# A streaming-encoder layer on one core: carrying the pacing of DRAM sums in small ScalarE copies, and one more plain tile in the first up product

## The chip, the cores and the metric

One core of a Trainium2 chip runs the whole layer in one launch. The metric is the device time of an execution in microseconds (us); the text also uses the span of the profiled execution, from its first to its last instruction.

## The reference

One macaron layer over 512 tokens of width 1024, in float32: `x += 1/2 SwiGLU(rms(x))`, `x += Mix(rms(x))`, `x += 1/2 SwiGLU(rms(x))`, `x = rms(x)`. SwiGLU is

```python
def swiglu_ffn(x, w_gate, w_up, w_down):
    return (jax.nn.silu(x @ w_gate) * (x @ w_up)) @ w_down   # w_gate, w_up: 1024x2816, w_down: 2816x1024
```

`Mix` is one input projection, chunked attention (8 heads of 64) beside a pooling mixer, and an output projection. The change touches the two SwiGLU blocks alone.

## The kernel before

**Precision.** Every operand is split in a high part (a copy rounded by ScalarE, L141 to L143, L684) and a low part (the rest, a subtraction on VectorE, L147 to L149). A product is three matmuls: high by high, high by low, low by high (`mm3`, L217 to L219, or `mm_part`, L226, which issues one of the three).

**The up product** (`ffn_up`, called once for each SwiGLU) makes 22 tiles of 128 hidden columns, each a gate and an up column block. The first `PLAIN[i]` tiles (L38: 5 in the first product, 4 in the second) are plain: 48 matmuls of 512 columns. Of those the first two are interleaved over four banks (`first`), the others take two 512 KB weight loads each. After them every tile is made by a Strassen-like scheme: seven half-size products, 84 matmuls of 256 columns, with the tokens' side in seven prepared blocks (A11, S1, S3, S2, A12, A22, S4; `Norm.blocks`, L538 on) and the weights' side in sums built on VectorE (L969 to L973).

**The planner.** Plain tiles and the next `LISTED` (8) half-size tiles are put in a list of jobs with costs. `Work.latest` gives each job a time by which it must have started, counted back from the matmuls in their fixed order; that becomes the rank of all ScalarE and VectorE jobs (L298, L299). `Work.plan` then runs the list through and emits each engine's instructions in the order that comes out, with limited rooms: 8 banks, 8 temporaries `t` of 128x512, 4 places for split weights (`part`), 2 and 2 for raw weights. The remaining tiles (9 in the first product, 10 in the second) are written out by hand in a loop (from L1159 on). The low part that the first of these tiles needs first may end 0.9 us after the last listed matmul (L1133 to L1135).

**The down product** needs four sums of blocks of the down weights, made in DRAM before it: 48 transfers (a copy, then an accumulating one, for 4 sums and 6 groups), issued by GpSimd. They are cut into portions. `Down.make_sums` (L1291) issues one portion: a one-column copy by GpSimd of some tile (`mark`, L1298), so that the portion starts when that tile has been written, and then the portion's transfers (L1300). GpSimd runs in order, and an accumulating transfer waits for the one below it. In the first product the 28 portions follow `norm.rb`, blocks S3, A11, S2, A22 and S1 (L927 to L938), the activation `sg` of plain tiles 2 to 4 (L879), the tile `u` of every listed half-size tile (L1094), `u` of every hand-written tile (L1194), and two products of the down stage. The second product has 16 portions in the mixer and 20 in the up product, on plain tiles 2 and 3 and the other 18 tiles. `sg` and `u` are temporaries `t`: their place can't be written again before GpSimd's one-column copy has read it.

**The start.** In the first product ScalarE squares the tokens (`square`, L740 on) for the mean that the norm needs; the squares may start as soon as the tokens and the gains are there.

Of the kernel before, what the change touches and what calls it, by code (L numbers as in the profile page):

```python
# [8 lines left out]
F32 = mybir.dt.float32  # L9
# [25 lines left out]
RAW = 2  # L35
HILO = 3
SHIFT = 16
PLAIN = (5, 4)  # L38
LISTED = 8
PROBS = 3  # L40
EARLY = 16
LATE = 4
# [15 lines left out]
UP_HOP = 0.2  # L58
FIRST_BYTE = 1.8
RAW_LAG = 8.0  # L60
MORE = 6
MIX_ENGINES = {
    mybir.EngineType.PE, mybir.EngineType.DVE, mybir.EngineType.Activation, mybir.EngineType.Pool,
}
# [2 lines left out]
def layer(  # L67
# [44 lines left out]
    def name(what):  # L112
        n_tiles[0] += 1
        return f"{what}_{n_tiles[0]}"
# [123 lines left out]
    class Job:  # L238
        def __init__(self, no, engine, cost, rank, emit, after, gets, uses, lag, chunk):
            self.engine, self.cost, self.rank, self.emit = engine, cost, rank, emit  # L240
            self.after = [z for z in after if z is not None]
            self.gets, self.uses, self.lag, self.chunk = list(gets), list(uses), lag, chunk
            self.no, self.then, self.waits, self.ready = no, [], len(self.after), 0.0
            self.spare, self.seat, self.t0 = 0.0, 0.0, None

    class Work:

# [15 lines left out]
        def latest(self, rooms):  # L263


            t, users, first = 0.0, {}, {}
            row = sorted((z for z in self.jobs if z.engine == "pe" and z.rank >= 10.0), key=lambda z: z.rank)
            for z in row:
                z.by = t
                t += z.cost  # L270
            for z in self.jobs:
                for key in z.uses:
                    users.setdefault(key, []).append(z)
                for what, key in z.gets:
                    if key not in first.setdefault(what, {}):
                        first[what][key] = z
            further = {}
            for what, n in rooms.items():
                got = first[what]
                if what == "bank":  # L280
                    keys = sorted(got, key=lambda key: getattr(got[key], "by", got[key].seat))
                else:
                    keys = list(got)
                for key, later in zip(keys, keys[n:]):
                    for z in users.get(key, ()):
                        further.setdefault(z.no, []).append(got[later])

            def start_by(z):
                if not hasattr(z, "by"):
                    z.by = None  # L290
                    ends = [start_by(k) - (0.0 if k.engine == z.engine else self.hop) for k in z.then + further.get(z.no, [])]
                    end = min([*ends, t + z.spare])
                    z.by = end - z.cost - z.lag
                return z.by

            for z in self.jobs:
                start_by(z)
                if z.engine in ("act", "dve"):  # L298
                    z.rank = z.by  # L299
            return t  # L300

        def plan(self, room, free):
# [327 lines left out]
    def ffn_up(norm, wA, down, loaded, in_order, plain, turns=(), early=()):  # L630
# [109 lines left out]
        def square(k, before):  # L740
            def first():
                norm.acc = tpool.tile([P, S], F32, tag="acc", name=name("acc"), bufs=1)
                nc.scalar.activation(norm.acc, x[k], AF.Square)

            def emit():
                nc.scalar.activation(buf["sq", k], x[k], AF.Square)

            def add():
                nc.vector.tensor_tensor(norm.acc, norm.acc, buf["sq", k], op=ALU.add)

            if before is None:
                return job("act", 0.56, rank["acc"], first, [at_x[k], gain_in])
            z = job("act", 0.56, rank["acc"] + k, emit, [at_x[k]], [("t", ("sq", k))])
            return job("dve", 0.61, rank["acc"] + k, add, [z, before], uses=[("sq", k)])

        def chunk(kp):
# [90 lines left out]

        placed = {}

        def add_sums(f, done):  # L850
            k, second = down.pair(f)
            if second:
                job("dve", 0.78, rank["second"], lambda: down.sums(f), [done, placed[k]])
            placed[k] = done

        def evacuate(n, f, gate, up, after):
            g, sg = ("g", n), ("sg", n)
            z = job(
                "dve", 0.62, rank["evac"],
                lambda: nc.vector.tensor_tensor(  # L860
                    natural(buf[g]), ordered(buf[gate]), natural(norm.rb), op=ALU.mult
                ),
                [at_rb, *after], [("t", g)], [gate],
            )
            z = job(
                "act", 0.57, rank["evac"], lambda: nc.scalar.activation(buf[sg], buf[g], AF.Silu),
                [z], [("t", sg)], [g],
            )
            z = job(
                "dve", 0.61, rank["evac"],  # L870
                lambda: nc.vector.tensor_tensor(buf[sg], buf[sg], norm.rb, op=ALU.mult), [z],
            )
            done = job(
                "dve", 0.61, rank["place"], lambda: down.place(f, ordered(buf[up]), buf[sg]), [z],
                uses=[up, sg],
            )
            add_sums(f, done)
            if n >= 2:
                job("pool", 3.2, n, lambda: down.make_sums(buf[sg]), [done])  # L879

        for i in range(2):
            evacuate(i, down.order[i], ("first", 2 * i), ("first", 2 * i + 1), at_first[2 * i : 2 * i + 2])
# [7 lines left out]
            job("pool", 2.8, 0, lambda k=k: put_aside(buf["turned", k], k), [z], uses=[("turned", k)], lag=3.5)  # L890

        freed = [None] * KD
        for n in range(2, plain):
            f, lows = down.order[n], []
            for j in range(2):
                key = ("W", n, j)
                kind = ("praw", "wraw")[j % 2 == 0]
                z = load(wA[2 * f + j], lambda key=key: buf[key][:, :1024], 0.45, 1.3, [(kind, key)])
                lows.append(
                    split_jobs(key, lambda key=key: buf[key][:, :1024], 1024, rank["plain"], [z], [key])  # L900
                )
            units = [(k, j) for k in range(KD) for j in range(2)]
            if n < plain - 1:
                units.sort(key=lambda u: u[1])
            last = [None] * 2
            for k, j in units:

                def unit(n=n, k=k, j=j):
                    w = buf["part", ("W", n, j)]()
                    mm3(buf["plain", n, j], cut(w, k * P, P), norm.h[k], k == 0, k == KD - 1)  # L910

                last[j] = job(
                    "pe", 0.648, filler(), unit, [lows[j][1], last[j]],
                    [("bank", ("plain", n, j))], [("part", ("W", n, j))],
                )
                if n == plain - 1 and j:
                    freed[k] = last[j]
            evacuate(n, f, ("plain", n, 0), ("plain", n, 1), last)
# [5 lines left out]
        used = {k: [turned[k]] if k in turned else [] for k in range(KD)}  # L924
        at_a = norm.blocks(down.pool, aside, work, at_rb, used, freed)

        if not loaded:  # L927
            for i, (z, after) in enumerate(
                (
                    (at_rb, lambda: norm.rb),  # L930
                    (at_a[S3][0][0], lambda: work.buf["whole", S3][0][:, 0].bitcast(F32)),
                    (at_a[A11][0][0], lambda: norm.a[A11][0][0].bitcast(F32)),
                    (at_a[S2][0][0], lambda: work.buf["whole", S2][0][:, 0].bitcast(F32)),
                    (at_a[A22][0][0], lambda: norm.a[A22][0][0].bitcast(F32)),
                    (at_a[S1][0][0], lambda: norm.a[S1][0][0].bitcast(F32)),
                )
            ):
                job("pool", 3.2, 1 + 0.1 * i, lambda after=after: down.make_sums(after()), [z])  # L938

        raws, w = {}, {}  # L940

# [84 lines left out]
        def operands(n):  # L1026
# [2 lines left out]
            raw = ("raw", n)  # L1029
            at_raw = job(  # L1030
                "sp", 0.9, n_loads[0] + n, lambda: fetch_into(buf[raw], down.order[n]), [],
                [("praw", raw)], lag=2.6 if n < plain + 2 else RAW_LAG,
            )

            def made(i, src, cols, deps, uses):
# [20 lines left out]
        def half_tile(n):  # L1056
# [34 lines left out]

            p = multiply(acc, 11, 0, A11, True, [])
            u_lo = read(u, 0, acc, 1.0, [p])
            job("pool", 3.2, n, lambda: down.make_sums(buf[u][:, :HT]), [u_lo])  # L1094
            p = multiply(up_hi, 13, S, S3, True, [])
            z_hi = read(z, 1, up_hi, -1.0, [p])
            p = multiply(acc, 24, 0, S2, False, [u_lo])
# [136 lines left out]
    class Down:  # L1234
# [56 lines left out]
        def make_sums(self, after):  # L1291

            at = self.n_sums
            self.n_sums += 1
            part = self.steps[self.bounds[at] : self.bounds[at + 1]]
            with tc.manual_schedule(engines={mybir.EngineType.Pool}):
                mark = small.tile([P, 16], F32, tag="mark", name=name("mark"))
                nc.gpsimd.tensor_copy(mark[:, 0:1], after[:, 0:1])  # L1298
                for _, at, i, g in part:
                    nc.gpsimd.dma_start(  # L1300
                        self.rows(i, g), self.rows(self.terms[i][at], g),
                        **(dict(accum_op=ALU.add) if at else {}),
                    )
# [1258 lines left out]
```

## Time and profile before

| | us |
|---|---|
| median of 3 runs | 806.54 (806.04 to 808.33) |
| profiled execution, its own time | 802.69 |
| span of that execution | 800.9 |

A row of the page or of a list of groups gives engine, line, operation and shape, then busy time and what ended the idle time before. A row of a timeline gives start, duration, engine and line; a bracket at its end is the idle time just before it and what ended it. TensorE is PE, its weight loads PEld, VectorE DVE, ScalarE ACT, GpSimd POOL.

### The profile page before, as it was taken

The page shows a single profiled execution, that of the slowest core. Times are in us where ns is not written, and L with a number is a line of the kernel's source. Part 1 is how long each engine was busy: PE and PEld are TensorE (multiplying, and loading weights), DVE is VectorE, ACT ScalarE, POOL GpSimd, SP SyncE. Part 2 cuts the span into 40 slices and gives each one's busy share as a digit, 9 for nine tenths or more (in the row PEclk, how much of TensorE's full clock was granted, in tenths as well). Part 3 has the DMA queues.
Part 4 walks back from the last instruction along what each step waited for, and adds up shares of the span by engine and source line. Part 5 has one row for each costly group of instructions (what it writes and reads, how often), then busy time and mean ns, then how long its engine had stood idle before and what let it go on. Part 6 is the DMA issues. An engine that isn't in the chain of part 4 may idle for free.

```text
span 800.9 us, 14970 instructions
## 1 busy us (share of the span) xinstructions
PE 790.1 (99%) x5706; PEld 746.2 (93%) x5706; DVE 712.4 (89%) x1117; ACT 498.7 (62%) x858; POOL 158.5 (20%) x246
## 2 busy tenths in 40 slices
PE   9999999999999999999999999999999999999996
PEld 7889899999999999888888888899999999988986
DVE  7899899999988998777699799999999999986997
ACT  7556565555666665557769555455666555766584
POOL 0035321122220000232254245021110011200010
PEclk9999999999999999999999999999999999999998
DMA  8469977698898765585655867145774467869642
GB/s 298 149 170 308 284 214 196 164 240 198 227 280 288 219 201 162 173 264 117 163 191 107 185 178 212 57 151 194 174 186 165 159 173 176 260 238 339 215 140 106
DMA packets 73992, 158.57 MB, mean 198 GB/s; under 512 B 6576, under 2 KB 31680, under 8 KB 73536
## 3 DMA queue, kind: packets, MB, share of 16 engines
q1 hardware_dynamic: 49952, 109.09, 40.3%
q0 software_dynamic: 23680, 48.24, 28.1%
q8 instruction: 45, 0.74, 0.4%
q10 hardware_dynamic: 288, 0.27, 0.1%
q14 instruction: 27, 0.22, 0.1%
HBM read 153.38 MB, written 50.34 MB: 254 GB/s over the span
## 4 chain that ended last, share of the span: by engine, by line
PE 85%; DVE 2%; DMA 1%; issue 1%; ACT 0%; SPq 0%; ACTq 0%; DVEq 0%
PE mm L217 12%; PE mm L219 12%; PE mm L218 12%; PE mm L226 10%; PE a L218 9%; PE a L217 9%; PE a L219 9%; PE a L226 6%; DMA raw<-wsum 1%; PE mm L2005 1%; PE mm L2095 1%; PE a L2069 1%; DVE parts L147 1%; PE mm L2069 0%; PE a L2095 0%
## 5 line engine op out<-in xcount | busy, mean ns | idle before, releaser
L147 DVE TENSOR_TENSOR parts<-raw,parts 128x1024 fp32r<-128x1024 f32 (+2 forms) x129 | 137.3, 1078 | 14.3 <-ACT parts L141 12.2
L1018 ACT ACTIVATE t<-mm 128x256 f32<-128x256 f32 x93 | 35.8, 385 | 86.6 <-PE mm L219 59.7
L141 ACT CAST parts<-raw 128x1024 fp32r<-128x1024 f32 (+1 forms) x60 | 59.3, 993 | 32.7 <-DMA raw<-wsum 10.3
L1298 POOL COPY mark<-t 128x1 f32<-128x1 f32 x40 | 24.9, 622 | 268.1 <-DVE t L1193 149.5
L1300 POOL DMA_DIRECT2D wsum<-in_wB_dram x72 | 73.0, 1146 | 12.6 <-DMA wsum<-wsum 7.5
L684 ACT CAST parts<-raw 128x1024 fp32r<-128x1024 f32 (+2 forms) x69 | 59.8, 883 | 17.8 <-PE a L218 8.0
L147 DVE TENSOR_TENSOR wlo<-raw,whi 128x1024 fp32r<-128x1024 f32 (+1 forms) x41 | 46.8, 1141 | 6.3 <-ACT whi L141 4.3
L147 DVE TENSOR_TENSOR ah<-acts,ah 128x512 fp32r<-128x512 f32 (+1 forms) x72 | 47.1, 663 | 3.0 <-ACT ah L141 2.9
L141 ACT CAST ah<-acts 128x512 fp32r<-128x512 f32 (+1 forms) x72 | 41.0, 583 | 8.6 <-PE mm L218 6.1
L219 PE MATMUL mm<-ha,parts 128*128 128x256 f32 x152 | 41.9, 276 | 0.8 <-DVE parts L147 0.8
L1598 DVE TENSOR_TENSOR parts<-raw,parts 128x1024 fp32r<-128x1024 f32 x24 | 29.6, 1239 | 14.7 <-ACT parts L1593 14.7
L217 PE MATMUL mm<-ha,parts 128*128 128x256 f32 x152 | 41.8, 275 | 0.0
L218 PE MATMUL mm<-ha,parts 128*128 128x256 f32 x152 | 41.8, 275 | 0.0
L1593 ACT CAST parts<-raw 128x1024 fp32r<-128x1024 f32 x24 | 25.2, 1048 | 25.9 <-PE a L218 7.1
L226 PE MATMUL mm<-ha,parts 128*128 128x256 f32 x312 | 38.6, 275 | 0.0
L217 PE MATMUL mm<-ah,parts 128*128 128x256 f32 x136 | 37.4, 275 | 0.0
L218 PE MATMUL mm<-ah,parts 128*128 128x256 f32 x136 | 37.4, 275 | 0.0
L219 PE MATMUL mm<-ah,parts 128*128 128x256 f32 x136 | 37.4, 275 | 0.0
L226 PEld LDWEIGHTS mm<-ha,parts 128*128 128x128 f32 x312 | 36.8, 192 | 0.1
L1018 ACT ACTIVATE t<-a 128x256 f32<-128x256 f32 x47 | 18.1, 384 | 29.5 <-PE a L226 21.2
L963 DVE TENSOR_TENSOR parts<-wsum,parts 128x1024 fp32r<-128x1024 f32 x26 | 31.7, 1219 | 2.6 <-ACT parts L958 2.6
L226 PE MATMUL a<-ha,parts 128*128 128x256 f32 x264 | 32.6, 275 | 0.0
(410 smaller groups left out, 3013.6 us busy)
## 6 DMA issues: line engine op xcount, KB each, us to landing
raw<-in_wA_dram SPq DMA_DIRECT2D x86, 512.0 KB, 5.1
wsum<-in_wB_dram POOLq DMA_DIRECT2D x60, 512.0 KB, 7.7
raw<-wsum SPq DMA_DIRECT2D x36, 512.0 KB, 4.9
raw<-in_wB_dram SPq DMA_DIRECT2D x30, 512.0 KB, 4.9
wsum<-wsum POOLq DMA_DIRECT2D x20, 512.0 KB, 4.8
x<-in_xT_dram SPq DMA_DIRECT2D x16, 256.0 KB, 5.3
raw<-in_wQK_dram SPq DMA_DIRECT2D x8, 512.0 KB, 4.1
wsum<-in_wB_dram POOLq DMA_DIRECT2D x12, 256.0 KB, 7.6
```

What stands on the lines that cost most here:

```text
L141: nc.scalar.copy(hi, src)
L147: nc.vector.tensor_tensor(lo, src, hi.bitcast(F32), op=ALU.subtract)
L217: nc.tensor.matmul(acc, a[0], high, start=start, stop=False, **more)
L218: nc.tensor.matmul(acc, a[0], low, start=False, stop=False, **more)
L219: nc.tensor.matmul(acc, a[1], high, start=False, stop=stop, **more)
L226: nc.tensor.matmul(acc, a[1 if i == 2 else 0], moved, start=start, stop=stop, **more)
L684: "act", c_high, rank_of, lambda: nc.scalar.copy(pair()[0], src()),
L963: nc.vector.tensor_tensor(lo, src, hi.bitcast(F32), op=ALU.subtract)
L1018: nc.scalar.activation(natural(dst), ordered(src), AF.Copy, scale=scale)
L1300: nc.gpsimd.dma_start(self.rows(i, g), self.rows(self.terms[i][at], g), **(dict(accum_op=ALU.add) if at else {}),)
L1593: return lambda: nc.scalar.copy(buf["part", i][0], buf["raw", i])
L1598: nc.vector.tensor_tensor(lo, buf["raw", i], hi.bitcast(F32), op=ALU.subtract)
```

## The change

Portions of the sums no longer read a temporary or a block. ScalarE copies one column of the tile in question to a tile of its own (`pace`, ring of 4), at once when that tile is written, and GpSimd's copy reads that. In the first product the portions now follow the high parts of seven weight tiles of the plain tiles (all but the first) and blocks S3, S2, A22 and S1; the three on `sg`, and those on `norm.rb` and A11, are gone. In the second they follow the high parts of the gate weights of plain tiles 2 and 3. `MORE` 7 for 6 makes 29 portions of the 28 in the first product. `PLAIN` becomes (6, 4) and `LISTED` 7: the first product has 6 plain, 7 listed and 9 hand-written tiles, the second 4, 7 and 11. Smaller parts: jobs of the norm's mean, of the tokens' split, of the squares and of the second to fourth weight tile rank 10 us earlier; the first two squares wait for split weights; the raw loads of the first two half-size tiles are planned with the same lag of 8.0 us as the others; `mark` has 8 columns, not 16.

```diff
-PLAIN = (5, 4)
-LISTED = 8
+PLAIN = (6, 4)
+LISTED = 7
...
-MORE = 6
+MORE = 7
+EARLY_MEAN = 10.0
...
                 if z.engine in ("act", "dve"):
-                    z.rank = z.by
+                    z.rank = -1e3 if z.at_once else z.by - EARLY_MEAN * (z.rank < -5.0 and z.rank >= -19.0)
...
             if before is None:
-                return job("act", 0.56, rank["acc"], first, [at_x[k], gain_in])
-            z = job("act", 0.56, rank["acc"] + k, emit, [at_x[k]], [("t", ("sq", k))])
+                return job("act", 0.56, rank["acc"], first, [at_x[k], at_w[0][0][0]])
+            then = at_w[0][3][0] if k == 1 else None
+            z = job("act", 0.56, rank["acc"] + k, emit, [at_x[k], then], [("t", ("sq", k))])
...
+        def pace(at, order, src):
+
+            n = next(paces)
+
+            def note():
+                buf["pace", n] = small.tile([P, 1], F32, tag="pace", name=name("pace"), bufs=4)
+                nc.scalar.copy(buf["pace", n], src())
+
+            z = job("act", 0.22, rank["copy"], note, [at])
+            z.at_once = True
+            job("pool", 3.2, order, lambda: down.make_sums(buf["pace", n]), [z])
...
             add_sums(f, done)
-            if n >= 2:
-                job("pool", 3.2, n, lambda: down.make_sums(buf[sg]), [done])
...
-        if not loaded:
-            for i, (z, after) in enumerate(
...
-                job("pool", 3.2, 1 + 0.1 * i, lambda after=after: down.make_sums(after()), [z])
+        at_weights = [z for pair in plain_lows[(0 if loaded else 1) :: (2 if loaded else 1)] for z in pair[:1]]
+        if loaded:
+            for i, (z, what) in enumerate(zip(at_weights, plain_keys[::2])):
+                pace(z, i, lambda what=what: buf["part", what](0, 0)[0][:, 0:1].bitcast(F32))
+        else:
+            for i, (z, what) in enumerate(zip(at_weights, plain_keys[1:])):
+                pace(z, i, lambda what=what: buf["part", what](0, 0)[0][:, 0:1].bitcast(F32))
+            for i, what in enumerate((S3, S2, A22, S1)):
+                pace(at_a[what][0][0], 10 + i, lambda what=what: norm.a[what][0][0][:, 0:1].bitcast(F32))
...
-                [("praw", raw)], lag=2.6 if n < plain + 2 else RAW_LAG,
+                [("praw", raw)], lag=RAW_LAG,
...
-            job("pool", 3.2, n, lambda: down.make_sums(buf[u][:, :HT]), [u_lo])
+            pace(u_lo, 20 + n, lambda: buf[u][:, 0:1])
...
-                mark = small.tile([P, 16], F32, tag="mark", name=name("mark"))
+                mark = small.tile([P, 8], F32, tag="mark", name=name("mark"))
```

## Rows read from the trace of the kernel before

**Rows 1.** The page: busy time of each engine, and its share of the span.

```profile
PE 790.1 (99%) x5706; PEld 746.2 (93%) x5706; DVE 712.4 (89%) x1117; ACT 498.7 (62%) x858; POOL 158.5 (20%) x246
```

**Rows 2.** Who TensorE waited for, whole span: us in total, times, longest.

```profile
PE mm L226 <- ACT t L1018: 1.9, 1, 1.9
PE a L448 <- DVE less_ln L432: 1.1, 1, 1.1
PE mm L219 <- DVE parts L147: 0.8, 1, 0.8
PE mm L226 <- ACT parts L684: 0.3, 1, 0.3
```

**Rows 3.** Stages: length, busy us (instructions) by engine, granted clock, DMA share, GB/s.

```profile
26.80:57.90 31.10, 31.10 (x146) 27.22 (x144) 29.87 (x38) 16.14 (x22) 8.65 (x12) 1.00 0.53 153
84.00:87.00 3.00, 1.11 (x10) 0.92 (x9) 1.52 (x3) 1.78 (x5) 2.51 (x6) 1.00 1.07 340
87.00:134.80 47.80, 47.80 (x430) 47.80 (x430) 46.55 (x70) 29.34 (x52) 12.60 (x16) 1.00 0.92 249
136.40:221.00 84.60, 84.60 (x758) 84.60 (x759) 80.13 (x113) 50.70 (x93) 17.09 (x26) 1.00 0.80 203
525.00:600.00 75.00, 75.00 (x674) 75.00 (x673) 71.27 (x102) 45.59 (x82) 15.95 (x22) 1.00 0.65 185
600.00:694.00 94.00, 94.00 (x843) 93.97 (x843) 88.79 (x126) 57.44 (x105) 12.82 (x22) 1.00 0.60 180
780.00:800.90 20.90, 14.47 (x99) 13.39 (x98) 15.77 (x48) 9.25 (x22) 0.00 (x0) 0.89 0.26 101
```

**Rows 4.** The chain that ended last: start, us, matmuls of 256 columns, then of 512.

```profile
107.11 6.70 PE mm L226 x60
...
489.23 15.11 PE mm L226 x70
```

**Rows 5.** Timeline of 77 to 91 us, all engines: before and after TensorE's longest stall.

```profile
77.05 2.48 POOL L1300 DMA_DIRECT2D wsum<-in_wB_dram  x1
...
84.49 0.51 POOL L1300 DMA_DIRECT2D wsum<-wsum  x1 [4.96 <-DMA wsum<-in_wB_dram]
84.98 0.20 POOL L1298 COPY mark<-t 128x1 f32<-128x1 f32 x1
...
85.22 0.42 ACT L1109 ACTIVATE t<-t 128x256 f32<-128x256 f32 x1 [3.96 <-POOL mark L1298]
85.54 0.60 ACT L684 CAST parts<-raw 128x512 fp32r<-128x512 f32 x1
...
86.75 1.60 PE L226 MATMUL mm<-sa,parts 128*128 128x256 f32 x12 [1.89 <-ACT t L1018]
```

**Rows 6.** Timelines of VectorE, then TensorE, at the end of the listed tiles.

```profile
134.13 0.42 DVE L1316 TENSOR_TENSOR acts<-acts 128x256 f32<-128x256 f32 x1
...
135.59 0.68 DVE L147 TENSOR_TENSOR parts<-raw,parts 128x512 fp32r<-128x512 f32 x1
136.19 1.22 DVE L147 TENSOR_TENSOR wlo<-raw,whi 128x1024 fp32r<-128x1024 f32 x1
...
136.32 0.38 PE L219 MATMUL mm<-ha,parts 128*128 128x256 f32 x1 [0.85 <-DVE parts L147]
```

**Rows 7.** Timelines of ScalarE and TensorE, 17 to 40 us: casts, first plain matmul, one-column activation.

```profile
18.66 1.03 ACT L684 CAST parts<-raw 128x1024 fp32r<-128x1024 f32 x1
...
26.82 0.38 PE L217 MATMUL a<-hhi,parts 128*128 128x512 f32 x1
...
30.08 0.20 ACT L441 ACTIVATE table<-t 128x1 f32<-128x1 f32 x1
...
37.16 1.05 ACT L684 CAST parts<-raw 128x1024 fp32r<-128x1024 f32 x1 [3.95 <-PE a L218]
```

**Rows 8.** DMA issues of 44 to 100, then 0 to 44 us: count, KB, us to landing.

```profile
wsum<-in_wB_dram POOLq DMA_DIRECT2D x15, 512.0 KB, 9.0
raw<-in_wA_dram SPq DMA_DIRECT2D x8, 512.0 KB, 7.3
...
raw<-in_wA_dram SPq DMA_DIRECT2D x12, 512.0 KB, 4.7
```

**Rows 9.** GpSimd's timeline, 0 to 260 us: the first portions of the sums.

```profile
29.34 1.11 POOL L1298 COPY mark<-rb 128x1 f32<-128x1 f32 x1 [27.54 <-DVE rb L534]
...
44.17 0.63 POOL L1298 COPY mark<-xa 128x1 f32<-128x1 f32 x1 [12.88 <-ACT xa L143]
```

**Rows 10.** Timeline of 0 to 10 us: TensorE and its weight loads at the start.

```profile
5.06 0.30 PEld L226 LDWEIGHTS mm<-hlo,parts 128*128 128x128 f32 x2 [0.24 <-DVE hlo L149]
...
7.83 0.48 PE L226 MATMUL mm<-hhi,parts 128*128 128x512 f32 x1 [0.34 <-ACT parts L684]
...
8.17 0.19 PEld L226 LDWEIGHTS mm<-hlo,parts 128*128 128x128 f32 x1 [0.16 <-DVE hlo L149]
```

**Rows 11.** VectorE's timeline around the end of the second product's listed tiles.

```profile
580.10 0.42 DVE L1086 TENSOR_TENSOR t<-a,t 128x256 f32<-128x256 f32 x1 [0.57 <-PE a L226]
...
598.54 0.68 DVE L147 TENSOR_TENSOR parts<-raw,parts 128x512 fp32r<-128x512 f32 x1
```

## What the change will do to the time

> **What bounds the kernel now.** I read the page's busy shares first. TensorE is busy 790.1 us of a span of 800.9, VectorE 89%, ScalarE 62%, GpSimd 20% [rows 1]. So the time is the sum of the matmuls plus 10.8 us in which TensorE stands still, and the next view is who it waited for [rows 2]: 1.9 us for ScalarE's reading of a bank (L1018), 1.1 before its first instruction, 0.8 for a low part from VectorE, 0.3 for a first cast. Third, the stages [rows 3]: the last 20.9 us hold 14.47 busy, so 6.43 of the idle time lies at the very end, out of the change's reach; 84 to 87 us has 1.11 busy of 3.00; the stretches beside it, and the whole of the second product's half-size tiles (525 to 694), are full. What the change can win is therefore bounded: 1.89 + 0.85 + 0.34 = 3.08 us. What it costs has to be looked for in matmuls, and in new stalls.
>
> **The longest stall, step by step** [rows 5]. GpSimd issues a transfer in 77.05 to 79.53, stands 4.96 us until one has landed, issues the accumulating one at 84.49, and only then makes its one-column copy (84.98). ScalarE's SiLU at L1109 wants a temporary `t` and waits 3.96 us for that copy. Behind it on ScalarE, which goes in order, stand a cast (85.54) and the bank readings L1116 and L1018; TensorE gets its bank at 86.75, having lost 1.89. So of a ScalarE wait of 3.96, 3.96 - 1.89 = 2.07 us was covered.
>
> **The other stall** [rows 6]. The third matmul of the first hand-written tile needs a 512-column low part; VectorE makes it at 135.59, after sums of activations (L1316) and other work, and TensorE loses 0.85. VectorE had been busy 46.55 of 47.80 us before that [rows 3]: it was late by its load.
>
> **The change, part by part.**
>
> *One half-size tile becomes a plain one.* Matmuls of 256 columns follow each other in 6.70 / 60 = 0.1117 us, those of 512 in 15.11 / 70 = 0.2159 [rows 4]. A half-size tile is 84 x 0.1117 = 9.38, a plain one 48 x 0.2159 = 10.36. The swap adds **0.98 us** to a TensorE that is full. The second product's swap is of a listed for a hand-written tile with the same 84 matmuls: 0. [...]
>
> *The portions' new source.* With `pace`, no temporary and no block waits for GpSimd any more in the listed tiles, so the wait of 3.96 has no cause left: **-1.89**. Bounds 0 (another late reader takes its place) and -1.89. I take the whole, since the copy's end at 85.18 is what stands right before the SiLU's start at 85.22.
>
> *What the copies cost ScalarE.* The first product gets 7 + 4 + 7 = 18, the second 2 + 7 = 9. A one-column activation takes 0.20 us [rows 7]: 27 x 0.20 = 5.4 us on an engine that is 29.34 of 47.80 busy among the half-size tiles [rows 3], so one copy in a tile lies in idle time: 0. If that cover went, a bank reading would be 0.20 late behind each copy. GpSimd gets one portion, so one `mark`, more; its transfers stay 48. Behind a copy that waits for its place in the ring of 4 stands all of ScalarE; that is a rival below.
>
> *When the transfers run.* The first portions come at 29.34 and 44.17 now [rows 9]; after the change they follow casts that are made from 18.66 on, at the first four intervals up to 37.16 one in 4.6 us [rows 7], so some seven portions run before 50 us, in a stretch where the DMA engines are only 0.53 busy [rows 3]. They share them with SP's weight loads. Where both were dense a weight load took 7.3 us to land [rows 8]. Plain weights are cast well ahead of use (18.66, the first matmul of their tile at 26.82 [rows 7]), so 0 on the path; between 0 and 7.3 - 4.7 = 2.6, if a load took that instead of the 4.7 of the first 44 us [rows 8] and nothing covered it. In exchange the pile-up of 60 to 85 us gets thinner.
>
> *VectorE's load.* A half-size tile takes it 46.55 x 9.38 / 47.80 = 9.13 us [rows 3]. A plain one takes two low parts of 1.22 and three operations of 512 columns at 0.68 [rows 6]: 4.48. The swap frees 4.65 us. The hand-over comes at 134.8 - 1.89 + 0.98 = 133.9, so 0.9 earlier, and VectorE was 0.85 late: 4.65 - 0.91 - 0.85 leaves 2.9 us of room if the freed time can be used. Part of it may fall before the tokens' blocks exist, when there is nothing to do. So between 0 and **-0.85**; I take the whole. The plain tile also puts 10.36 us between the start and the first half-size tile, which can only help the blocks.
>
> *Hand-over in the second product.* It comes a tile earlier, at some 590.7. VectorE waited 0.57 us for TensorE at 580.10, so it had no arrears there, and its low part for the hand-over at 600.1 was made from 598.54 to 599.22 [rows 11]. I take 0, between 0 and +0.85, the stall of the first product.
>
> *The start.* The first squares move behind casts. TensorE's 0.34 at 7.83 was ended by such a cast [rows 10]; but its next weight load at 8.17, like that at 5.06, waited for a low part of the tokens from VectorE, which nothing moves. So 0, between 0 and -0.34. Earlier ranks for the norm's mean make `rb` earlier; no TensorE wait hangs on it [rows 2]: 0. The lag of 8.0 and the narrower `mark`: 0, no row has a wait that they would move.
>
> **Sum**: 0.98 - 1.89 - 0.85 = -1.76 us. Against the profiled execution's 802.69 that is 800.9; the median of the runs shown is 806.54, 3.85 above it, and -1.76 on that gives **804.8**. That is 0.22%; about 0.3%, 2.4 us, is what a measurement of this kernel can tell from no change.
>
> **Rivals.**
>
> *Only the GpSimd stall goes.* VectorE's freed time falls into the plain tiles, where its work waits for raw weights and for places, and the 0.85 stays: 0.98 - 1.89 = -0.91, 805.6. For it: VectorE is 96% busy in 26.8 to 57.9 only while blocks are made [rows 3], and these keep their place beside the last plain tile. Against it: the second product, with one tile more in its list, had no such stall [rows 3].
>
> *It doesn't do what it says.* The releaser in the trace is inferred; if the temporary was late for another reason as well, the 1.89 stays: 0.98 - 0.85 = +0.13, 806.7, or with both stalls +0.98, 807.5. Against it: those 0.04 us between the copy's end and the SiLU [rows 5].
>
> *More is won.* The start's 0.34 as well, and in the executions that aren't profiled a wait for GpSimd that is longer than the 3.96 here, since it hangs on when transfers land: every further microsecond of it counts in full, as the 2.07 of cover are used up. With 0.34 and half a microsecond: -2.6, 803.9.
>
> *Slower: ScalarE waits for the ring.* A `pace` copy can't be written before GpSimd has read the one four before. Portions come every 4.6 us in the plain tiles [rows 7], and a portion whose accumulating transfer waits for one just issued takes up to a landing, 9.0 us [rows 8]. While such portions alternate with free ones GpSimd is two to three portions behind; from four on ScalarE stands. One whole landing, less the cover of 2.07 seen above, is 6.9 us: -1.76 + 6.9 = +5.2, 811.7. Against it: the cover is larger among plain tiles, whose casts are 8 us ahead. [...]
>
> **Chances.** Forecast 0.42, only one stall gone 0.13, nothing gone 0.15, more won 0.18, ring 0.12. The forecast's own range, with a microsecond of spread between medians, is 803.5 to 806.2. The range to the neighbours, leaving out most of the ring's case and the tail of the gains, is **802.6 to 808.6**. Faster by over 0.3% takes a third of the forecast, most of "more won" and little else: 0.32. Slower: the ring and a part of "nothing gone": 0.17. Within 0.3%: 0.51.
>
> **What would show it.** TensorE's instructions fall by 36 and its busy time rises by about 1; no TensorE wait for L1018 near 85 to 97 us, no ScalarE wait for `mark`; GpSimd's first `mark` near 19 us; no wait for `parts` at the hand-over near 134 us; nothing new at 590. Wrong would be: a ScalarE wait for `mark` at the pace copies, a TensorE stall among plain tiles 3 to 5 for weights, or one at 590.

## The result, and the profile after

The changed kernel takes 811.57 us (median of six runs, 809.93 to 812.73), the kernel before 806.04 beside it (median of five): a ratio of 1.0065 (95% interval 1.0042 to 1.0088), 0.65% slower. Two slow executions far outside the rest, one of 888.49 us of the kernel before and one of 1672.07 us in the last experiment below, are left out of the medians. The forecast was 804.8, in a range of 802.6 to 808.6.

First the waits of TensorE in the profile after, the view of [rows 2], and the first line of the page:

```profile
PE 794.6 (98%) x5670; PEld 747.4 (92%) x5670; DVE 709.0 (87%) x1111; ACT 501.8 (62%) x878; POOL 154.3 (19%) x247
```

```profile
PE mm L219 <- DVE parts L1612: 7.0, 1, 7.0
PE a L449 <- DVE less_ln L433: 1.1, 1, 1.1
PE a L219 <- DVE wlo L148: 0.8, 1, 0.8
PE mm L227 <- ACT parts L685: 0.3, 1, 0.3
PE mm L220 <- DVE parts L148: 0.3, 1, 0.3
PE a L518 <- DVE t L829: 0.2, 1, 0.2
```

(Line numbers are those of the changed kernel, some 1 to 14 further on; L1612 is the mixer's low part, `low_part`.) Of the two stalls that the prediction wanted to remove, the 1.89 at the bank reading is off the list, and of the 0.85 at the hand-over 0.3 is left (L220 waiting for `parts`, at 135.13 us). New is one of 7.0 us in a stage that the change doesn't touch: the mixer, which begins after the first down product.

The timeline of TensorE after, at the mixer's start (L218 to L220 on `parts,hhi` are its first matmuls, L518 on `m,mean_of` is a later landmark):

```profile
323.16 0.38 PE L218 MATMUL mm<-parts,hhi 128*128 128x512 f32 x1
330.50 0.80 PE L219 MATMUL mm<-parts,hhi 128*128 128x512 f32 x1 [6.95 <-DVE parts L1612]
331.09 0.63 PE L220 MATMUL mm<-parts,hlo 128*128 128x512 f32 x1
334.93 0.54 PE L220 MATMUL mm<-parts,hlo 128*128 128x512 f32 x1
335.30 0.38 PE L218 MATMUL mm<-parts,hhi 128*128 128x512 f32 x1
346.31 0.59 PE L518 MATMUL a<-m,mean_of 128*128 128x512 f32 x2
```

The same landmarks before:

```profile
323.80 0.38 PE L217 MATMUL mm<-parts,hhi 128*128 128x512 f32 x1
337.40 0.59 PE L517 MATMUL a<-m,mean_of 128*128 128x512 f32 x2
```

The reader sees where 10.0 us of span (810.9 against 800.9) come from. At the mixer's first matmul the changed kernel is 323.80 - 323.16 = 0.64 *ahead*. From there to the landmark it takes 23.15 and not 13.60, 9.55 more: the stall of 6.95, and the eleven matmuls from 330.50 to 335.30, which take 4.80 where 11 x 0.2159 [rows 4] = 2.37 would do. The windows say why those are slow (columns: stretch, its length, busy and instructions, granted clock, share of DMA, GB/s):

```profile
328.00:330.00 2.00, 0.00 (x0) 0.60 0.00 0
332.00:334.00 2.00, 2.00 (x6) 0.50 0.87 285
335.00:336.00 1.00, 1.00 (x6) 0.88 0.35 143
```

The rest, 1.09, comes later; 0.79 of it is the wait of `wlo` at 749.65.

**Who was late.** ScalarE and VectorE at the mixer's start, after (L1607 is the mixer's cast, L1612 its low part; L1428 adds a product to the tokens, L512 sums their squares):

```profile
321.91 1.05 ACT L1607 CAST parts<-raw 128x1024 fp32r<-128x1024 f32 x1 [7.31 <-PE a L219]
322.69 1.43 DVE L1428 SCALAR_TENSOR_TENSOR x<-a,x 128x256 f32<-128x256 f32 x4 [6.93 <-PE a L220]
328.62 0.69 DVE L512 TENSOR_TENSOR acc<-acc,t 128x512 f32<-128x512 f32 x1
329.23 2.35 DVE L1612 TENSOR_TENSOR parts<-raw,parts 128x1024 fp32r<-128x1024 f32 x2
```

and before:

```profile
317.19 1.05 ACT L1593 CAST parts<-raw 128x1024 fp32r<-128x1024 f32 x1 [1.43 <-PE a L218]
318.27 1.23 DVE L1598 TENSOR_TENSOR parts<-raw,parts 128x1024 fp32r<-128x1024 f32 x1 [1.72 <-ACT parts L1593]
319.87 1.05 ACT L1593 CAST parts<-raw 128x1024 fp32r<-128x1024 f32 x1 [1.63 <-PE a L218]
320.95 1.23 DVE L1598 TENSOR_TENSOR parts<-raw,parts 128x1024 fp32r<-128x1024 f32 x1 [1.45 <-ACT parts L1593]
323.33 1.43 DVE L1414 SCALAR_TENSOR_TENSOR x<-a,x 128x256 f32<-128x256 f32 x4 [1.16 <-PE a L219]
```

Before, two of the mixer's weights are split while TensorE still does the down product, and the tokens' sums come behind them. After, the first cast waits 7.31 us for a matmul of the down product to let its place go, and the low part stands on VectorE behind the tokens' work of 322.69 to 329.23.

**Theory P, the places.** Split weights go round in four places: the mixer's three of `parts_sb` and one in a pool. A plain tile asks for two of them, a half-size one for four, and the down product goes on from where the up product stopped. Counted in the code, the tiles and the down product ask 120 times before, 118 times after. 120 is a multiple of four and 118 is two off, so after the change the last down weights lie in other places. The mixer always begins with places 0, 1, 2. Before, the weight in place 0 was the first of the last ones to be used up; after, it is one of the last two. **Rival L:** the mixer's loads or the portions are late by the new timing. In the profile after, no transfer runs at all from 322 to 331 (a share of 0.00 in every window there), so the loads are not merely slow; but they too wait for room, and the rows alone don't separate cause from effect.

### The profile page after: what moved, and what is told of

Its sections match the earlier page's. It is cut to its first block, busy times and chain, and to the rows that moved or that the text cites. A ratio compares the mean times of both kernels' runs of the same rounds, so it can differ in the third digit from the quotient of the medians.

```text
span 810.9 us, 14852 instructions
## 1 busy us (share of the span) xinstructions
PE 794.6 (98%) x5670; PEld 747.4 (92%) x5670; DVE 709.0 (87%) x1111; ACT 501.8 (62%) x878; POOL 154.3 (19%) x247
## 4 chain that ended last, share of the span: by engine, by line
PE 92%; DVE 4%; DMA 2%; ACT 1%; issue 1%; SPq 0%; DVEq 0%; ACTq 0%
PE mm L220 13%; PE mm L218 13%; PE mm L219 13%; PE mm L227 12%; PE a L218 10%; PE a L220 10%; PE a L219 10%; PE a L227 8%; DMA wsum<-wsum 1%; PE mm L2019 1%; PE mm L2109 1%; PE a L2083 1%; DVE parts L148 1%; DMA raw<-in_wA_dram 1%; DVE parts L977 1%
## 5 line engine op out<-in xcount | busy, mean ns | idle before, releaser
L1032 ACT ACTIVATE t<-mm 128x256 f32<-128x256 f32 x88 | 33.9, 386 | 86.3 <-PE mm L220 63.0
L142 ACT CAST parts<-raw 128x1024 fp32r<-128x1024 f32 (+1 forms) x62 | 61.2, 993 | 33.6 <-PE mm L219 10.9
L685 ACT CAST parts<-raw 128x1024 fp32r<-128x1024 f32 (+2 forms) x65 | 56.2, 885 | 24.3 <-PE a L219 10.9
L977 DVE TENSOR_TENSOR parts<-wsum,parts 128x1024 fp32r<-128x1024 f32 x36 | 43.9, 1220 | 5.0 <-ACT parts L972 5.0
L1607 ACT CAST parts<-raw 128x1024 fp32r<-128x1024 f32 x24 | 25.1, 1046 | 35.2 <-PE a L219 11.1
L1312 POOL COPY mark<-pace 128x1 f32<-128x1 f32 x27 | 14.8, 548 | 161.9 <-ACT pace L858 161.9
L148 DVE TENSOR_TENSOR wlo<-raw,whi 128x1024 fp32r<-128x1024 f32 (+1 forms) x37 | 41.9, 1133 | 3.9 <-ACT whi L685 2.2
L1612 DVE TENSOR_TENSOR parts<-raw,parts 128x1024 fp32r<-128x1024 f32 x24 | 29.4, 1232 | 18.2 <-ACT parts L1607 18.2
L220 PE MATMUL mm<-ha,parts 128*128 128x256 f32 x160 | 44.2, 276 | 0.2
L218 PE MATMUL mm<-ha,parts 128*128 128x256 f32 x160 | 44.0, 275 | 0.0
L219 PE MATMUL mm<-ha,parts 128*128 128x256 f32 x160 | 44.0, 275 | 0.0
L220 PE MATMUL mm<-ah,parts 128*128 128x256 f32 x148 | 40.8, 276 | 0.3 <-DVE parts L148 0.3
L218 PE MATMUL mm<-ah,parts 128*128 128x256 f32 x148 | 40.7, 275 | 0.0
L219 PE MATMUL mm<-ah,parts 128*128 128x256 f32 x148 | 40.7, 275 | 0.0
L1312 POOL COPY mark<-t 128x1 f32<-128x1 f32 x20 | 6.1, 303 | 166.4 <-DVE t L1207 166.4
L1032 ACT ACTIVATE t<-a 128x256 f32<-128x256 f32 x48 | 18.5, 386 | 28.5 <-PE a L227 20.2
L972 ACT CAST parts<-wsum 128x1024 fp32r<-128x1024 f32 x36 | 35.7, 1044 | 0.0
```

Source lines behind the costliest of these rows:

```text
L142: nc.scalar.copy(hi, src)
L148: nc.vector.tensor_tensor(lo, src, hi.bitcast(F32), op=ALU.subtract)
L218: nc.tensor.matmul(acc, a[0], high, start=start, stop=False, **more)
L219: nc.tensor.matmul(acc, a[0], low, start=False, stop=False, **more)
L220: nc.tensor.matmul(acc, a[1], high, start=False, stop=stop, **more)
L685: "act", c_high, rank_of, lambda: nc.scalar.copy(pair()[0], src()),
```

## The experiments

**The mixer's places alone.**

```diff
+        own_places = (2, 0, 1)
         def part_at(slot):
-            return parts_sb[:, slot * 2112 :][:, :1024], ...
+            at = own_places[slot] * 2112
+            return parts_sb[:, at:][:, :1024], ...
...
-            own_order[kp] = work.slot_of["part", "up", kp][1]
+            own_order[kp] = own_places[work.slot_of["part", "up", kp][1]]
```

> The changed kernel, but the mixer takes its first three split weights' places in the order 2, 0, 1 instead of 0, 1, 2 (place 2 holds the down weight that is multiplied earliest of those left, place 0 one that is multiplied nearly last). Theory P (places: with one half-size tile fewer the rotation of four places ends two further on, so the mixer's first cast asks for a place that the down product still reads): ScalarE's first mixer cast comes near 317 to 319 us instead of 321.9 behind a wait of 7.3, TensorE's stall of 6.95 at 330.5 is below 1.5, the clock of 0.50 to 0.69 behind it is gone (some 2.3 us), and the time falls by 7 to 9.5, to 802 to 804.5. Rival L (the mixer's loads, or the portions, come late by the new timing): the cast still waits 5 us or more and the time stays within 1.5 of 811.6.

Measured: 803.57 us (803.14 to 804.17), 0.9972 of the kernel before (0.9958 to 0.9986; its median beside it 806.06), 8.0 below the changed kernel. Its timeline:

```profile
315.70 1.05 ACT L1610 CAST parts<-raw 128x1024 fp32r<-128x1024 f32 x1 [1.96 <-PE a L219]
321.06 1.05 ACT L1610 CAST parts<-raw 128x1024 fp32r<-128x1024 f32 x1 [4.31 <-PE a L219]
328.38 2.35 DVE L1615 TENSOR_TENSOR parts<-raw,parts 128x1024 fp32r<-128x1024 f32 x2
329.65 0.48 PE L219 MATMUL mm<-parts,hhi 128*128 128x512 f32 x1 [1.78 <-DVE parts L1615]
```

One permutation of three places takes the loss away. The stall of 1.78 that remains (expected: below 1.5) belongs to the second weight: its cast is over at 322.11, but its low part stands behind the tokens' sums until 328.38. Rival L falls.

**The copies without the plain tile.** The changed kernel with the tile numbers of before:

```diff
-PLAIN = (6, 4)
-LISTED = 7
+PLAIN = (5, 4)
+LISTED = 8
...
-MORE = 7
+MORE = 6
```

> The changed kernel with the numbers of before: five plain and eight listed half-size tiles in the first product, six listed portions; the small copies, the portions' new sources and the edits at the start stay. Theory P: the places end as before, so no TensorE stall above 1 at the mixer's start; the 1.89 is still gone, the start's 0.73 stays: about -1.2 against the kernel before, 804 to 806 timed (profiled 801 to 802). Rival L, the portions or the new copies make the mixer late: a stall of 5 to 7 near 330 and 810 to 813.

Measured: 801.18 us (800.80 to 801.85), 0.9952 of the kernel before (0.9935 to 0.9968): the fastest so far, and more than either theory gave. Its waits of TensorE hold no mixer:

```profile
PE a L449 <- DVE less_ln L433: 1.1, 1, 1.1
PE a L219 <- DVE wlo L148: 0.7, 1, 0.7
PE mm L220 <- DVE parts L148: 0.4, 1, 0.4
```

On the profile's scale, 799.0 against 800.9, the gain is about the 1.89 of the prediction. On the scale of the timed runs it is 806.06 - 801.18 = 4.88. The difference lies in the kernel before, not in this one (below).

**The plain tile without the copies.** The kernel before with the tile numbers of after:

```diff
-PLAIN = (5, 4)
-LISTED = 8
+PLAIN = (6, 4)
+LISTED = 7
```

> The kernel before with six plain and seven listed half-size tiles in the first product and nothing else of the change: no small copies, portions still follow the temporaries. Theory P: the stall of the changed kernel appears, 5 to 7 us before the mixer's first weights and some 2 us of half and 0.69 clock behind it, ScalarE's first mixer cast near 322 behind a wait of TensorE; 811 to 815 timed. Rival L: no such stall; the swap's 0.98 alone or less, 805.5 to 807.5.

Measured: 811.87 us, 1.0087 (1.0067 to 1.0106). Two of its four waits of TensorE, its first mixer cast, GpSimd's longest wait in the listed tiles, and all that ScalarE waits for GpSimd:

```profile
PE mm L218 <- DVE parts L1598: 7.0, 1, 7.0
PE mm L226 <- DVE parts L147: 0.3, 1, 0.3
```

```profile
321.49 1.05 ACT L1593 CAST parts<-raw 128x1024 fp32r<-128x1024 f32 x1 [7.32 <-PE a L218]
88.11 0.51 POOL L1300 DMA_DIRECT2D wsum<-wsum  x1 [8.25 <-DMA wsum<-in_wB_dram]
```

```profile
ACT t L1018 <- POOL mark L1298: 0.2, 1, 0.2
```

The stall comes with the tile and needs none of the copies. What was not expected: its list of waits has no bank reading (L1018) any more, so the long stall of before goes without any copy. GpSimd itself is no earlier: it stands 8.25 us and reads a `t` at 88.61, later than the kernel before at its stall (84.98 [rows 5]), but ScalarE waits only 0.2 us for a `mark`. Why that late reading holds up nothing here isn't shown; the order of the portions has changed (the first two that read a `t` come at 55.87 and 59.29, before at 65.46 and 73.27). The two parts of the change remove the same stall; their gains do not add up, and with the copies on top (811.57) the kernel is no faster than with the tile alone.

**A second profile of the kernel before**, unchanged.

> The kernel before, unchanged, for a second profile: its unprofiled runs (803.99 to 808.33) are longer than its profiled 802.69, and the trace does not show where. If the mixer's start is what varies, this profile has a stall above 1 us near 331 with a lower clock behind it and a time between 803 and 808; if the difference is spread or lies at the end, no single new stall above 0.5.

Measured: 806.77 us, a span of 805.0. Waits of TensorE:

```profile
PE mm L226 <- ACT t L1018: 3.8, 1, 3.8
PE a L448 <- DVE less_ln L432: 1.1, 1, 1.1
PE mm L219 <- DVE parts L147: 0.7, 1, 0.7
PE a L226 <- ACT t L1018: 0.2, 1, 0.2
```

GpSimd's wait ahead of the first of these, and windows behind it (it ends at 89.58):

```profile
87.31 0.51 POOL L1300 DMA_DIRECT2D wsum<-wsum  x1 [6.76 <-DMA wsum<-in_wB_dram]
```

```profile
90.00:92.00 2.00, 2.00 (x11) 0.50 0.94 318
92.00:94.00 2.00, 2.00 (x18) 0.87 1.10 249
```

Neither expectation held: there is one longer stall, but at the bank reading, not at the mixer. It is the stall of [rows 5], 3.80 and not 1.89, because GpSimd stands 6.76 us on the landing of the transfer below, not 4.96. Behind this stall the granted clock was 0.50, in the window of 90 to 92; behind the 1.89 of [rows 2] it was 1.00 [rows 3]. From the first half-size tile to the mixer this execution takes 327.85 - 58.19 = 269.66, that of the prediction 323.80 - 57.90 = 265.90. Of the 3.76 more, 1.92 are stalls (3.80 + 0.18 + 0.68 against 1.89 + 0.85) and 1.84 are left. The lower clock shows in 1.28 of these: the first 12 matmuls behind the stall take 92.30 - 89.58 = 2.72 us here, and 88.19 - 86.75 [rows 5] = 1.44 in the profile of the prediction. This execution first, then that one:

```profile
89.58 2.93 PE L226 MATMUL mm<-sa,parts 128*128 128x256 f32 x12 [3.80 <-ACT t L1018]
92.30 0.94 PE L226 MATMUL mm<-ha,parts 128*128 128x256 f32 x6
```

```profile
88.19 1.50 PE L226 MATMUL mm<-ha,parts 128*128 128x256 f32 x12
```

So the profile on which the prediction rested was a mild execution of before. In this one the two stalls at the bank reading and these 1.84 come to 3.80 + 0.18 + 1.84 = 5.82, three times the 1.89.

**Before, with unfavourable places.** In the kernel before, `own_places = (2, 1, 0)` with the other edits of the first experiment, so that nothing but the place of the mixer's weights moves.

> The kernel before with the mixer's places in the order 2, 1, 0 instead of 0, 1, 2 and nothing else, so that its first split weight asks for the place whose down weight is multiplied nearly last. Nothing before the mixer moves. Theory P: ScalarE's first mixer cast waits for TensorE to within 2 us of the down product's end, TensorE stalls 3 to 7 us at the mixer's first weights and its clock falls behind it; 809 to 814. Rival (the changed kernel's stall came with the plain tile in another way, by timing or load): no stall above 1, 805 to 807.

Measured: 808.16 us (805.52 to 811.43), 1.0034 of before (1.0014 to 1.0055; its median beside it 805.21). The profiled execution, 811.43, is the longest of the ten; it has stalls of 3.97 and 1.02 at the bank reading as well. Timeline of the mixer's start:

```profile
327.17 2.00 ACT L1596 CAST parts<-raw 128x1024 fp32r<-128x1024 f32 x2 [6.79 <-PE a L218]
329.29 1.22 DVE L1601 TENSOR_TENSOR parts<-raw,parts 128x1024 fp32r<-128x1024 f32 x1
330.56 0.48 PE L218 MATMUL mm<-parts,hhi 128*128 128x512 f32 x1 [1.76 <-DVE parts L1601]
336.94 0.48 PE L218 MATMUL mm<-parts,hhi 128*128 128x512 f32 x1 [0.93 <-DVE parts L1601]
```

The cast is as late as after the change (a wait of 6.79), with every tile as before: the place makes it late. But the time is below the 809 of the expectation, TensorE loses 1.76 + 0.93 = 2.69, not 6.95, and its matmuls from 330.88 to 335.63 follow each other in 4.75 / 22 = 0.2159 us, the pitch of [rows 4]. Here VectorE has the first low part right behind the tokens' products and ahead of the sums; after the change it stood behind both. A late place alone costs some 3 us here (808.16 - 805.21 = 2.95). The rest of the changed kernel's loss goes with VectorE's other order; that the order makes it, and what gives the build that order, isn't shown.

**Seven plain tiles.** Two half-size tiles made plain against before ask for 2 x (4 - 2) = 4 places fewer: a whole turn.

```diff
-PLAIN = (6, 4)
-LISTED = 7
+PLAIN = (7, 4)
+LISTED = 6
...
-MORE = 7
+MORE = 8
```

> The changed kernel with seven plain and six listed half-size tiles (one portion more, as it has one more source). Two half-size tiles fewer than before shift the rotation by four places, a whole turn. Theory P: no stall above 1 at the mixer's start; against the kernel with five plain tiles and the same copies (801.18) two swaps more at 0.98 less a hand-over stall of 0.40 that goes: 802 to 803.5, faster than the changed kernel by 8 or more although it has one slower tile more. Rival (a plain tile more makes the mixer late): stall of 7 or more, 812 to 814.

Measured: 802.13 us (801.83 to 803.93), 0.9962 of before (0.9947 to 0.9978), 9.4 below the changed kernel with one costly tile more. All of its waits of TensorE:

```profile
PE a L449 <- DVE less_ln L433: 1.1, 1, 1.1
```

Six tiles stall at the mixer, five and seven don't: a plain tile more is not by itself what makes the mixer late; the phase in which it leaves the ring is. Against five tiles this is +0.95; the two swaps at 0.98, less the stalls of 0.40 and 0.69 that stood in the one profile of five, are +0.87.

**The copies of the listed tiles alone.** The kernel before with `pace`, a `mark` of 8 columns and this line:

```diff
-            job("pool", 3.2, n, lambda: down.make_sums(buf[u][:, :HT]), [u_lo])
+            pace(u_lo, n, lambda: buf[u][:, 0:1])
```

> The kernel before with small copies for the listed half-size tiles alone (and the mark of 8 columns, which makes the room for them); other sources, tiles and start as before. If the long stall hangs on GpSimd holding the temporaries u of listed tiles: no TensorE wait for the bank reading, a hand-over stall of 0.4 to 0.9 stays, 801 to 802.5. If the early portions on weights and the edits at the start carry the gain instead: the stall of 2 to 4 stays and the time is 805 to 807.

Measured: 805.58 us, 1.0011 (0.9996 to 1.0027), no gain. The stall is as in the second profile of before (L1032 is its bank reading, L1123 the SiLU):

```profile
87.22 0.51 POOL L1314 DMA_DIRECT2D wsum<-wsum  x1 [6.44 <-DMA wsum<-in_wB_dram]
87.72 0.20 POOL L1312 COPY mark<-t 128x1 f32<-128x1 f32 x1
87.96 0.42 ACT L1123 ACTIVATE t<-t 128x256 f32<-128x256 f32 x1 [5.55 <-POOL mark L1312]
89.49 2.93 PE L226 MATMUL mm<-sa,parts 128*128 128x256 f32 x12 [3.48 <-ACT t L1032]
```

The `mark` that ScalarE waits for reads a `t`, not a `pace`. In this kernel only the portions of plain tiles read a `t` there: the temporary held is the `sg` of a plain tile and not the `u` of a listed tile. It is the third such portion, so by their order the `sg` of the last plain tile, which VectorE multiplied last in 78.24 to 78.92; GpSimd, in arrears, reads it at 87.72, some 9 us later.

**The start.** The kernel of five plain tiles with the ranks of the norm's mean and the conditions of the first squares as before:

```diff
-z.rank = -1e3 if z.at_once else z.by - EARLY_MEAN * (...)
+z.rank = -1e3 if z.at_once else z.by
...
-return job("act", 0.56, rank["acc"], first, [at_x[k], at_w[0][0][0]])
+return job("act", 0.56, rank["acc"], first, [at_x[k], gain_in])
...
-z = job("act", 0.56, rank["acc"] + k, emit, [at_x[k], then], ...)
+z = job("act", 0.56, rank["acc"] + k, emit, [at_x[k]], ...)
```

> The kernel with five plain tiles and the small copies (801.18), with the edits at the start undone: ranks of the norm's mean and the first squares as before. If they are worth nothing within 0.5: first half-size tile at 57.6 to 58.3 (57.76 with them, 57.90 and 58.19 in two profiles of the kernel before), 800.7 to 801.7. If they cost the 0.7 that the changed kernel's first half-size tile was late: 800 to 800.7, and that tile below 57.4.

Measured: 800.86 us (median of seven, 800.03 to 802.64), 0.9954 of before (0.9935 to 0.9973), against 801.18 and 0.9952 with the edits: worth nothing that shows. When the first half-size tile starts in this kernel isn't known. In the changed kernel's profile the first half-size tile came at 69.00, later than 57.90 + 10.36 = 68.26; the same start in the first experiment gave 68.46, so most of that 0.74 was this one execution.

## Why the prediction was wrong, step by step

**The step that failed: "One half-size tile becomes a plain one".** The prediction read its matmuls right (36 fewer; with seven plain tiles two swaps less two stalls were worked out as +0.87, and +0.95 was measured) and took them for the whole price: "The swap adds 0.98 us to a TensorE that is full." It did not ask which other thing the tiles count out. The tile also hands on the ring of split weights in another phase, across a down product, to a stage 190 us later. That cost 6.95 of stall and some 2.4 of clock (4.80 - 2.37). Shown: by the places alone (-8.0), by the tile alone (the same stall), by seven tiles (none), by unfavourable places in the kernel before (the late cast back, with 2.69 of stall). The list of what would make the prediction wrong looked no further than the up products, so the true case stood in no rival; 0.17 for slower was too little and for other reasons. The rival of the ring came to 811.7, next to the 811.57 measured; that is chance, as no copy waits for its place in the ring.

**The removed stall: right in place, too small, and gone for two reasons.** It went, as forecast. With five plain tiles it goes with the new sources of the early portions, among which `sg` no longer is, and not through the copies of `u`: copies of the listed tiles alone keep it, and the edits at the start are worth nothing. With six it goes without any copy. Its -1.89 came from the mildest of the four profiles that have it; the others lost 3.80 + 0.18, 3.97 + 1.02 and, with some copies, 3.48 + 0.83. TensorE was slower behind the long stall in these as well: its first 24 matmuls take 4.41 us in the second of these three (89.89 to 94.30) and 4.40 in the third (89.49 to 93.89), against 2.78 in the mildest (86.75 to 89.53). The runs of before spread over 802.36 to 809.27; those of the kernel with five tiles, in whose profile ScalarE and TensorE wait for GpSimd nowhere, over 800.80 to 801.85. The rival "More is won" had the right mechanism, that every further microsecond counts in full (ScalarE's waits of 5.87 and 5.55 left TensorE 3.80 and 3.48, each 2.07 less, as the 3.96 left 1.89), and gave it half a microsecond. The gap of 3.85 between the profiled execution and the median was added back as if nothing in it could be won; by the one second profile it was mostly this stall. With the sizes that the runs show, -4.88 for the copies, +0.98 for the tile and 9.38 for stall and clock make +5.5; 811.57 - 806.04 = 5.53.

**What held.** The first `mark` comes at 21.83 (forecast: near 19) and seven portions come before 50 us, as worked out:

```profile
21.83 0.36 POOL L1312 COPY mark<-pace 128x1 f32<-128x1 f32 x1 [20.03 <-ACT pace L858]
45.92 1.40 POOL L1312 COPY mark<-pace 128x1 f32<-128x1 f32 x1
```

The copies cost ScalarE little, 27 of them at 0.19 us (14 of a `t`, 7 of `parts` and 6 others), and the ring of four never held it: no wait of ScalarE for GpSimd is left in the profile, so the rival "ScalarE waits for the ring" did not happen (with seven plain tiles a copy waited once, 0.4 us). The marks of the hand-written tiles, 20 in both products, still read a `t` after the change, and no wait hangs on them.

```profile
L858 ACT COPY pace<-t 128x1 f32<-128x1 f32 x14 | 2.7, 191 | 1.1
L858 ACT COPY pace<-parts 128x1 f32<-128x1 f32 x7 | 1.3, 192 | 0.3
```

VectorE's hand-over went in the larger part, 0.59 of the 0.85: the third matmul there (135.13) follows the second (134.76) by 0.37, 0.26 above the pitch of 0.11, which is the 0.3 in the list of waits after. With five tiles 0.40 stays; in the first experiment and with seven tiles none is listed. The second product's hand-over cost 0, as taken. "The start: 0" held in the times.

**Left open.** That the rest of the changed kernel's mixer stall is VectorE's order is read from the rows of two kernels whose orders differ in other ways as well; a kernel with the late place and the early low part, all else as after, wasn't tried. The 0.7 to 1.0 that TensorE waits for a `wlo` near 740 stands in three of the profiles (after, five tiles, unfavourable places) and not in the others, though the first experiment and the two profiles of before have the same tiles in the second product as these; what makes it wasn't looked for.

## What to carry to other kernels

A change of how many pieces a stage has also changes where a rotating set of buffers stands when the stage ends: count the allotments modulo the ring, up to the next stage that begins at a fixed place, before taking the stages behind for unchanged. Where a profiled execution is well below the median, look for the wait that depends on a transfer's landing (here 4.96 us in one profile and 6.76 in the next), and price it from a second profile. The copies without the extra plain tile are the version to keep: 0.9952 of the kernel before.

## What was not expected of the hardware

The longer stalls cost more than their own length, as TensorE was slower behind them. Behind 1.89 [rows 5] and 1.78 (the first experiment) the granted clock was 1.00, and behind 1.76 (unfavourable places) the matmuls kept the pitch of 0.2159; behind 3.80 and 6.95 the clock was 0.50, until about 93 and 335 us. The first 12 matmuls behind the 3.80 took 1.28 us more than those behind the 1.89, and the eleven behind the 6.95 took 2.43 more than at the pitch of [rows 4]:

```profile
330.00:331.00 1.00, 1.00 (x6) 1.00 0.28 74
```

is the window of the first experiment right behind its stall, to be held against 332 to 334 us after the change. The matmuls from 331.09 to 334.93 follow each other in 3.84 / 9 = 0.427 us, 1.98 times the 0.2159 of [rows 4], at half the granted clock.
